# Rope, turns, values and the v0 bank in the attention loop of a hybrid decoder layer

## The chip, the cores and the metric

The kernel runs on one core of a Trainium2 chip. The core has five engines that work side by side and meet through semaphores: TensorE (PE in the profile, with its weight loads as PEld), VectorE (DVE), ScalarE (ACT), GpSimd (POOL) and SyncE (SP), whose queue issues the DMAs here. Matmuls and transposes write to PSUM, a memory of eight banks of 128 x 512 fp32; the other data lies in SBUF. The metric is the time of one execution on the device in microseconds (us).

## The reference

One layer of a hybrid decoder, all in fp32, for one sequence of 512 positions and a model width of 1024:

```python
h = rms_norm(x, norm_w)
u_s, z_s, q, k, v, z_a, r_s, r_a = split(h @ w_in)        # 1024 x 9216
y_s = s5_branch(u_s, ...)                                  # complex diagonal state space, GELU, GLU
y_s = (y_s * silu(z_s)) @ w_ssm_out
q = rope(rms_norm(q, q_norm_w)); k = rope(rms_norm(k, k_norm_w))   # 3 groups x 8 heads x 64
y_a = dilated_attention(q, k, v)       # windows 128, 512, 2048 at dilations 1, 4, 16
y_a = (y_a * silu(z_a)) @ w_attn_out
m = sigmoid(r_s) * y_s + sigmoid(r_a) * y_a
x = x + m @ w_o
```

The rope turns the first 16 of the 64 elements of each head of q and k: halves x1, x2 become x1 cos - x2 sin and x2 cos + x1 sin. The three groups' attention outputs are combined by their softmax denominators.

## The kernel before

**Matmuls.** fp32 accuracy comes from splitting both operands into a rounded part (`hi`) and a rest (`lo`) and making three matmuls, hi x hi, hi x lo and lo x hi (`mm3`, lines 62 to 65). Weights come from HBM by `load_w` (from line 183): SP's queue loads a piece, ACT rounds it to `w_hi` (line 108), DVE subtracts it to `w_lo` (line 110). There are two buffers of raw weights and three each of `w_hi` and `w_lo`; `get_w` hands out the next piece of a fixed list and starts the load of the piece two further on.

**Before the loop**, up to about 397 us: the norm of x, the state space branch, gates, and the projections by w_glu and w_ssm_out. Then the attention, by pairs of heads (`hp`, 0 to 3), each with its three groups.

**The loop** (from line 1094) does for each pair `hp`:

- `scores`: score matmuls in banks `sps`, softmax on DVE and ACT (lines 929 and 931), the merge of the groups' statistics, with small copies on POOL (lines 961 and 978), and the scaling of the probabilities `Pt` on DVE (line 985).
- `qk_first` for the next pair: a granule, that is `wide_granule` (line 817), q and k of groups 0 and 1 by 1024 rows of weights in four quarters. A quarter `kq` takes one piece of weights and runs four blocks, one for each 128 positions `r`, of six matmuls each into the four accumulators `pj`. The granule's result is copied to `raws` by ACT and goes through `qk_norm` (line 834): root mean square and scaling on DVE (line 846, 1024 elements a group), then the rope, four operations on POOL for each group (lines 852 to 857).
- `qk_second`: a second granule, q and k of group 2 and v of groups 1 and 2. Its callback `mid(kq)` runs in front of each quarter: in front of the second, `qk_turn` of group 0; in front of the third, `qk_turn` of group 1 (inside `queued()`); in front of the last, `values` of the present pair. The accumulators are emptied by ACT (lines 903, 905, squares at 879).
- `v0_unit`: v of group 0 for the next pair, 24 matmuls into an accumulator `pj`, then a copy `vt`; then `qk_turn` of group 2, and the transposes of `vt` (`finv`).

The last pair has no next one: it runs gate projections (`ra_unit`) and its `values`.

**A turn** (`qk_turn`, line 859) makes the transposed q (a = 0) and k (a = 1) of a group: for each of q and k four transposes of 128 x 128 into one bank `qtp`, which ACT copies to the rounded part (line 873) and DVE to the rest (line 874); the bank comes free behind both. For k of groups 1 and 2 the copies are made in two halves of 64 partitions.

**`values`** (line 988) takes the pair's probabilities in four steps: for each of the two heads, up to four transposes into a bank `ptp` and a copy of it to SBUF, `ptb`, by ACT for the first head (line 1027) and by DVE for the second (line 1029); then, one step behind, 16 matmuls of 128 columns into the bank `ot`. Together 30 transposes and 60 matmuls.

**PSUM** in this part (lines 1041 to 1043): four accumulators `pj` (pool `ps_p`), three banks for turns, scores, `ptp` and the transposes of v0 (pool `ps_g`, function `bank`), one for `ot`.

**Order.** A planner orders the instructions of each engine when the program is built, by the order in which the program names them and a model of their costs; an instruction that isn't ready by the model lets later ones pass. Each engine then runs its list in that fixed order. `queued()` (line 69) ties the instructions traced inside it, on PE, behind the PE instruction traced last.

Of the kernel before, what the change touches and what calls it, by code (L numbers as in the profile page):

```python
# [2 lines left out]

# [1 line left out]

# [6 lines left out]
F32 = mybir.dt.float32  # L12
# [3 lines left out]
ALU = mybir.AluOpType  # L16
# [17 lines left out]
NP = 4  # L34
# [18 lines left out]
def tile_hybrid_block(ctx: ExitStack, tc: tile.TileContext, x, positions, norm_w, w_in, lam_re, lam_im,  # L53
# [15 lines left out]
    def queued():  # L69

        return tc.issue_after(last[0].ins)
# [28 lines left out]
    def bank(name):  # L100
        return ps_g.tile([P, 512], F32, name=name, tag="g")
# [90 lines left out]
        split(hi, lo, raw, lo_eng=lo_w[0])  # L192
        return hi, lo

    def cm_unit(rh, rl, kts=KT):
        hi, lo = get_w()
        ps = ps_p.tile([P, 512], F32, name="pj", tag="pj")
        for k in range(kts):
            mm3(ps, hi[:, k], lo[:, k], rh[:, k], rl[:, k], k == 0, k == kts - 1)
        return ps  # L200
# [380 lines left out]
                            hi[:, k], lo[:, k], kh == 0 and k == 0 and rr == 0, kh == 1 and k == 3)  # L581
        return pss

    def v0_unit(hp, V):
        ps = cm_unit(hT_hi, hT_lo)
        vt = t2k("vt")
        act.copy(vt.rearrange("p (b r j) -> p r b j", r=4, b=4), ps.rearrange("p (r b j) -> p r b j", r=4, b=4))

        def finish():
            pt = bank("vtp")  # L590
            for b in range(NB):
                pe.transpose(pt[:, b * P:(b + 1) * P], vt[:, b * P:(b + 1) * P], ident)
            act.copy(V[:, 0].rearrange("p b c -> p (b c)"), pt)
        return finish
# [219 lines left out]
    if "gT" in dbg:  # L814
        sp.dma_start(dbg["gT"], gT_hi.bitcast(F32).rearrange("p k s -> p (k s)"))

    def wide_granule(th, tl, mid=None):

        pss = [ps_p.tile([P, 512], F32, name="pj", tag="pj") for _ in range(NB)]
        for kq in range(4):  # L820
            if mid:
                mid(kq)
            hi, lo = get_w()
            for r in range(NB):
                for k in range(2):
                    kk = 2 * kq + k
                    mm3(pss[r], th[:, kk, r * P:(r + 1) * P], tl[:, kk, r * P:(r + 1) * P], hi[:, k], lo[:, k],
                        kk == 0, kk == KT - 1)
        return pss

    def new_raw(i):
# [2 lines left out]
    def qk_norm(gs, raws, sq):  # L834

        n = 4 * len(gs)
        v = sml.tile([P, 32], F32, name="qv", bufs=1)[:, 0:NB * n]
        rstd = sml.tile([P, 32], F32, name="qrstd", bufs=1)[:, 0:NB * n]
        qa = sml.tile([P, 32], F32, name="qa", bufs=1)[:, 0:NB * n]
        qb = sml.tile([P, 32], F32, name="qb", bufs=1)[:, 0:NB * n]  # L840
        dve.tensor_scalar(v.rearrange("p (r h) -> p r h", r=NB), sq, 1.0 / HD, EPS, op0=ALU.mult, op1=ALU.add)
        rsqrt(rstd, v, [P, NB * n], qa, qb)
        rs = rstd.rearrange("p (r h) -> p r h", r=NB)
        for i, (g, raw) in enumerate(zip(gs, raws)):
            rv = raw.rearrange("p r (h d) -> p r h d", h=4)
            dve.tensor_tensor(rv, rv, rs[:, :, 4 * i:4 * i + 4].unsqueeze(3).broadcast_to([P, NB, 4, HD]), op=ALU.mult)  # L846
            t1 = sml.tile([P, NB * 2, 2, 16], F32, name="rt1", bufs=1)
            t2 = sml.tile([P, NB * 2, 2, 16], F32, name="rt2", bufs=1)
            rh = raw.rearrange("p r (a h d) -> p (r a) h d", a=2, h=2)
            cv = tC[:, g].rearrange("p r a d -> p (r a) d").unsqueeze(2)  # L850
            sv = tS[:, g].rearrange("p r a d -> p (r a) d").unsqueeze(2)
            pool.tensor_tensor(t1, rh[:, :, :, 0:16], cv.broadcast_to([P, NB * 2, 2, 16]), op=ALU.mult)  # L852
            pool.tensor_tensor(t2[:, :, :, 0:8], rh[:, :, :, 8:16],
                               sv[:, :, :, 0:8].broadcast_to([P, NB * 2, 2, 8]), op=ALU.mult)
            pool.tensor_tensor(t2[:, :, :, 8:16], rh[:, :, :, 0:8],
                               sv[:, :, :, 8:16].broadcast_to([P, NB * 2, 2, 8]), op=ALU.mult)
            pool.tensor_tensor(rh[:, :, :, 0:16], t1, t2, op=ALU.add)

    def qk_turn(g, raw, QT, KA, KB):
        for a in range(2):  # L860
            ps = bank("qtp")
            pn = ps.rearrange("p (b r j) -> p r b j", r=4, b=4)
            for r in range(NB):
                o = pn[:, r] if g == 0 else ps[:, r * P:(r + 1) * P]
                pe.transpose(o, raw[:, r, a * P:(a + 1) * P], ident)
            if a == 0 or g == 0:
                parts = [(slice(0, P), QT[0][:, g], QT[1][:, g]) if a == 0 else (slice(0, P), KA[0], KA[1])]
            else:
                parts = [(slice(64 * h, 64 * h + 64), KB[0][64 * h:64 * h + 64, g - 1, h],
                          KB[1][64 * h:64 * h + 64, g - 1, h]) for h in range(2)]  # L870
            for sl, hi, lo in parts:
                w = wcol[sl, g, a:a + 1]
                act.activation(hi, ps[sl], AF.Copy, scale=w)  # L873
                dve.scalar_tensor_tensor(lo, ps[sl], w, hi.bitcast(F32), op0=ALU.mult, op1=ALU.subtract)  # L874
# [18 lines left out]
        qk_norm((0, 1), raws, sq)  # L893
        return raws

    def qk_second(hp, mid=None):

        pss = wide_granule(hT_hi, hT_lo, mid)
        raw = new_raw(0)
        V = new_v()  # L900
        sq = sml.tile([P, NB, 8], F32, name="ssq")[:, :, 0:4]
        for r in range(NB):
            act.copy(raw[:, r], pss[r][:, 0:256])
            squares(sq[:, r], pss[r][:, 0:256])
            act.copy(V[:, 1:3, r], pss[r][:, 256:512].rearrange("p (g c) -> p g c", g=2))  # L905
        qk_norm((2,), [raw], sq)
        return raw, V
# [80 lines left out]
    def values(hp, Pt, V):  # L988
        ot = ps_o.tile([P, 512], F32, name="ot", tag="o")
        ov = ot.rearrange("d (r b j) -> d b r j", r=4, b=4)  # L990
        pend = []

        def pv(kind, bb, pts):
            for i in range(2):
                b = 2 * bb + i
                for k in range(2):
                    if kind == 0 and b == 0 and k == 0:
                        continue
                    for h in range(2):
                        po = slice(64 * h, 64 * h + 64)  # L1000
                        if kind == 0:
                            v = V[:, 0, b - 1 + k, po]
                            o = ov[po, b]
                        else:
                            v = V[:, 1 + k, b, po]
                            o = ot[po, b * P:(b + 1) * P]
                        first = kind == 0 and b == 0
                        pe.matmul(o, v, pts[h][:, (2 * i + k) * P:(2 * i + k + 1) * P], start=first,
                                  stop=kind == 1 and b == NB - 1 and k == 1, skip_group_check=True)

        n = 0
        for kind in range(2):
            for bb in range(2):
                pts = []
                k0 = 1 if kind == 0 and bb == 0 else 0
                for h in range(2):
                    ps = bank("ptp")
                    for i in range(2):
                        for k in range(2):
                            if 2 * i + k < k0:  # L1020
                                continue
                            pe.transpose(ps[:, (2 * i + k) * P:(2 * i + k + 1) * P],
                                         Pt[:, h, kind, 2 * bb + i, k * P:(k + 1) * P], ident)
                    pt = PT[n % 4]
                    n += 1
                    if h == 0:
                        act.copy(pt[:, k0 * P:], ps[:, k0 * P:])
                    else:
                        dve.tensor_copy(pt[:, k0 * P:], ps[:, k0 * P:])
                    pts.append(pt)  # L1030
                pend.append((kind, bb, pts))
                if len(pend) > 1:
                    pv(*pend.pop(0))
        pv(*pend.pop(0))
        at = t2k("at")
        dve.scalar_tensor_tensor(at, ot, 0.5, sza[:, hp], op0=ALU.mult, op1=ALU.mult)
        split(aT[:, 0, hp], aT[:, 1, hp], at, lo_eng=pool)
# [56 lines left out]
    for hp in range(NP):  # L1094
        Pt = scores(hp, *QK)
        if hp < NP - 1:
            raws = qk_first()

            def mid(kq):
                if kq == 1:  # L1100
                    qk_turn(0, raws[0], *QK)
                if kq == 2:
                    with queued():
                        qk_turn(1, raws[1], *QK)
                if kq == 3:
                    values(hp, Pt, V)

            raw, V_next = qk_second(hp + 1, mid)
            V = V_next
            finv = v0_unit(hp + 1, V)  # L1110
            qk_turn(2, raw, *QK)
            finv()
        else:
# [68 lines left out]
```

## Time and profile before

| what | value |
|---|---|
| median of 3 runs | 728.95 us (727.94 to 730.92) |
| profiled execution | 727.79 us |
| its span, first to last instruction | 726.0 us |
| mean granted TensorE clock | 0.991 |
| busy PE, DVE, ACT, POOL | 691.6, 455.4, 314.6, 190.9 us |
| HBM read and written | 68.46 and 10.49 MB |

A row of a timeline gives start, duration of the run of instructions, engine, line, operation, tile written and tiles read, shapes and count; in brackets the engine's idle time before it and who ended it. A row of a window gives its length and, for PE, PEld, DVE, ACT and POOL, busy us and (in brackets) instructions, then the granted PE clock, the DMA engines' busy share and GB/s. A row of groups gives count, busy us, mean ns of one, and the engine's idle time before them. A row of waits gives us in total, times, longest. Matmuls are pipelined, so their durations overlap: what one costs in a stream is the distance of starts.

### The profile page before, as it was taken

What the parts mean: (1) busy time and instruction counts of PE and PEld (TensorE: products, weight loads), DVE (VectorE), ACT (ScalarE), POOL (GpSimd) and SP (SyncE); (2) the same over time, 40 slices, a digit from 0 to 9 for tenths busy, and PEclk for the clock granted to TensorE, in tenths of its full rate; (3) what the DMA queues carried; (4) which work ended last, traced back from release to release, by engine and by line L of the source; (5) the groups of instructions that cost most, each with busy time, mean ns of one, the idle gap of its engine ahead of it and who ended that gap; (6) DMA issues with size and microseconds to landing.
All of it is one profiled execution on the core that took longest, in us unless ns stands there. A gap on an engine that the chain in (4) does not pass through costs nothing.

```text
span 726.0 us, 12680 instructions
## 1 busy us (share of the span) xinstructions
PE 691.6 (95%) x4821; PEld 574.3 (79%) x4821; DVE 455.4 (63%) x912; ACT 314.6 (43%) x631; POOL 190.9 (26%) x346
## 2 busy tenths in 40 slices
PE   2799799999999999999999999999989998999997
PEld 2787687788978887888889888788868877888886
DVE  6859663999956645764325659755764667464832
ACT  6433453332326465442144456537253725443320
POOL 3426540140205343450000326121601160230000
PEclk9999899999999999999999999999999999999999
DMA  8433652564546544455333432322312231327441
GB/s 206 106 99 93 169 135 79 142 159 132 122 131 147 127 105 138 129 166 185 95 102 94 131 88 63 84 59 59 115 32 60 62 112 30 116 74 249 130 145 58
DMA packets 137213, 82.14 MB, mean 113 GB/s; under 512 B 32696, under 2 KB 125632, under 8 KB 137024
## 3 DMA queue, kind: packets, MB, share of 16 engines
q1 hardware_dynamic: 135088, 78.96, 38.0%
q0 software_dynamic: 2048, 2.36, 2.6%
q8 instruction: 38, 0.62, 0.4%
q14 instruction: 23, 0.19, 0.1%
q10 hardware_dynamic: 16, 0.00, 0.0%
HBM read 68.46 MB, written 10.49 MB: 109 GB/s over the span
## 4 chain that ended last, share of the span: by engine, by line
PE 89%; DVE 3%; ACT 2%; SPq 2%; DMA 2%; issue 1%; ACTq 0%
PE pj L63 73%; PE sps L63 3%; PE yps L63 3%; PE ot L63 2%; PE ptp L67 2%; PE kps L63 2%; PE xps L63 1%; DMA Uj<-ud 1%; PE qtp L67 1%; SPq L443 1%; PE wps L67 1%; DVE w_lo L110 1%; DMA w_raw<-in_w_in_dram 1%; ACT qkp L873 1%; SPq L219 1%; ACT w_hi L108 1%
## 5 line engine op out<-in xcount | busy, mean ns | idle before, releaser
L108 ACT ACTIVATE w_hi<-w_raw 128x1024 fp32r<-128x1024 f32 x100 | 106.1, 1062 | 231.8 <-PE pj L63 197.4
L110 DVE TENSOR_TENSOR w_lo<-w_raw,w_hi 128x1024 fp32r<-128x1024 f32 x98 | 124.5, 1271 | 106.5 <-ACT w_hi L108 106.0
L63 PE MATMUL pj<-hT_lo,w_hi 128*128 128x512 f32 (+1 forms) x344 | 130.9, 381 | 3.6 <-DVE hT_lo L252 3.6
L63 PE MATMUL pj<-hT_hi,w_hi 128*128 128x512 f32 (+1 forms) x344 | 130.8, 383 | 2.0 <-ACT V L905 1.4
L63 PE MATMUL pj<-hT_hi,w_lo 128*128 128x512 f32 (+1 forms) x344 | 130.7, 381 | 1.6 <-DVE w_lo L110 1.6
L63 PE MATMUL pj<-w_hi,hT_hi 128*128 128x512 f32 (+1 forms) x288 | 105.6, 368 | 0.0
L63 PE MATMUL pj<-w_lo,hT_hi 128*128 128x512 f32 (+1 forms) x288 | 105.6, 367 | 0.0
L63 PE MATMUL pj<-w_hi,hT_lo 128*128 128x512 f32 (+1 forms) x288 | 105.2, 368 | 0.0
L63 PEld LDWEIGHTS pj<-hT_lo,w_hi 128*128 128x128 f32 x344 | 65.5, 190 | 15.6 <-DVE hT_lo L252 4.5
L63 PEld LDWEIGHTS pj<-hT_hi,w_lo 128*128 128x128 f32 x344 | 65.5, 190 | 14.4 <-DVE w_lo L110 2.6
L63 PEld LDWEIGHTS pj<-hT_hi,w_hi 128*128 128x128 f32 x344 | 65.1, 191 | 14.5 <-ACT V L905 2.1
L63 PEld LDWEIGHTS pj<-w_hi,hT_lo 128*128 128x128 f32 x288 | 54.3, 189 | 8.8
L63 PEld LDWEIGHTS pj<-w_hi,hT_hi 128*128 128x128 f32 x288 | 54.3, 189 | 8.8 <-issue 0.2
L63 PEld LDWEIGHTS pj<-w_lo,hT_hi 128*128 128x128 f32 x288 | 54.4, 189 | 8.6
L931 ACT ACTIVATE Pt<-Pt,st 128x256 f32<-128x256 f32 (+1 forms) x64 | 31.0, 492 | 18.4 <-DVE st L929 18.4
L852 POOL TENSOR_TENSOR rt<-qraw,tC 128x256 f32<-128x256 f32 x12 | 14.1, 1175 | 86.8 <-DVE qraw L846 86.5
L735 POOL TENSOR_TENSOR kt<-kt,dg 16x128 f32<-16x128 f32 x8 | 4.8, 597 | 120.7 <-ACT kt L734 116.2
L739 POOL DMA_DIRECT2D dd<-kt x64 | 33.7, 535 | 2.4 <-POOL kt L735 2.4
L874 DVE SCALAR_TENSOR_TENSOR qkp<-qtp,wcol,qkp 128x512 fp32r<-128x512 f32 (+1 forms) x32 | 23.0, 746 | 12.7 <-ACT qkp L873 12.7
L961 POOL COPY sw<-st 32x4 f32<-32x4 f32 x64 | 12.0, 187 | 71.4 <-ACT Pt L931 68.6
L873 ACT ACTIVATE qkp<-qtp,wcol 128x512 fp32r<-128x512 f32 (+1 forms) x32 | 20.8, 685 | 15.2 <-PE qtp L67 10.0
L278 POOL TENSOR_TENSOR ab<-dd,AT 128x512 f32<-128x512 f32 x16 | 22.0, 1385 | 14.1 <-DVE ab L279 14.1
(263 smaller groups left out, 1289.0 us busy)
## 6 DMA issues: line engine op xcount, KB each, us to landing
w_raw<-in_w_in_dram SPq DMA_DIRECT2D x40, 512.0 KB
w_raw<-in_w_in_dram SPq DMA_DIRECT2D x112, 128.0 KB
w_raw<-in_w_glu_dram SPq DMA_DIRECT2D x8, 512.0 KB
w_raw<-in_w_ssm_out_dram SPq DMA_DIRECT2D x8, 512.0 KB
w_raw<-in_w_o_dram SPq DMA_DIRECT2D x8, 512.0 KB
x_all<-in_x_dram SPq DMA_DIRECT2D x4, 512.0 KB
ud<-uT SPq DMA_DIRECT2D x8, 256.0 KB
Uj<-ud SPq DMA_DIRECT2D x8, 256.0 KB
```

Of the source, the lines that this page charges most:

```text
L63: last[0] = nc.tensor.matmul(*a, **k)
L67: last[0] = nc.tensor.transpose(*a, **k)
L108: act.activation(hi, src, AF.Copy, scale=scale)
L110: e.tensor_tensor(lo, src, hi.bitcast(F32), op=ALU.subtract)
L219: sp.dma_start(x_t[r], xv[r])
L278: eng.tensor_tensor(tv, a2.unsqueeze(2).broadcast_to(sh), ai, op=ALU.mult)
L739: pool.dma_start(M[Q * t:Q * t + Q, :, 0:P - Q * t], kt[:, :, t:].rearrange("q g k p -> q g (k p)"))
L852: pool.tensor_tensor(t1, rh[:, :, :, 0:16], cv.broadcast_to([P, NB * 2, 2, 16]), op=ALU.mult)
L873: act.activation(hi, ps[sl], AF.Copy, scale=w)
L874: dve.scalar_tensor_tensor(lo, ps[sl], w, hi.bitcast(F32), op0=ALU.mult, op1=ALU.subtract)
L931: act.activation(o, o, AF.Exp, bias=nm, scale=-1.0, accum_out=st[:, kind, 1, h, b:b + 1])
L961: pool.tensor_copy(sw[32 * r:32 * r + 32, :, :, b], st[32 * b:32 * b + 32, 1, :, :, r])
```

## The change

Five things change in the loop.

1. The four rope operations go from POOL to DVE, in all groups.
2. `wide_granule` calls `mid(kq, r)` in front of every block instead of every quarter, and a new callback `after(kq, r)` behind it. When `mid` says so, the block's matmuls are tied behind the PE instruction traced last.
3. The turns of groups 0 and 1 are each cut into their q and k: q of group 0 stands in front of the third quarter's last block, k of group 0, q of group 1 and k of group 1 in front of the last quarter's first, second and third block. Each is tied behind the PE instruction in front of it, and the block behind it is tied too.
4. `values` is traced behind the second quarter's last block instead of in front of the last quarter. For all pairs but the last, ACT makes both heads' copies to `ptb`.
5. `v0_unit` in the loop accumulates in a bank of the turns' pool instead of an accumulator `pj`.

```diff
-    def cm_unit(rh, rl, kts=KT):
+    def cm_unit(rh, rl, kts=KT, ps=None):
         hi, lo = get_w()
-        ps = ps_p.tile([P, 512], F32, name="pj", tag="pj")
+        if ps is None:
+            ps = ps_p.tile([P, 512], F32, name="pj", tag="pj")
...
-    def wide_granule(th, tl, mid=None):
+    def wide_granule(th, tl, mid=None, after=None):
...
         for kq in range(4):
-            if mid:
-                mid(kq)
             hi, lo = get_w()
             for r in range(NB):
-                for k in range(2):
-                    kk = 2 * kq + k
-                    mm3(pss[r], th[:, kk, r * P:(r + 1) * P], tl[:, kk, r * P:(r + 1) * P], hi[:, k], lo[:, k],
-                        kk == 0, kk == KT - 1)
+                tied = mid(kq, r) if mid else False
+                with queued() if tied else nullcontext():
+                    for k in range(2):
+                        kk = 2 * kq + k
+                        mm3(pss[r], th[:, kk, r * P:(r + 1) * P], tl[:, kk, r * P:(r + 1) * P], hi[:, k], lo[:, k],
+                            kk == 0, kk == KT - 1)
+                if after:
+                    after(kq, r)
...
-            pool.tensor_tensor(t1, rh[:, :, :, 0:16], cv.broadcast_to([P, NB * 2, 2, 16]), op=ALU.mult)
+            dve.tensor_tensor(t1, rh[:, :, :, 0:16], cv.broadcast_to([P, NB * 2, 2, 16]), op=ALU.mult)
...
-    def qk_turn(g, raw, QT, KA, KB):
-        for a in range(2):
+    def qk_turn(g, raw, QT, KA, KB, turned=(0, 1)):
+        for a in turned:
...
-                    if h == 0:
+                    if h == 0 or hp < NP - 1:
                         act.copy(pt[:, k0 * P:], ps[:, k0 * P:])
...
-            def mid(kq):
-                if kq == 1:
-                    qk_turn(0, raws[0], *QK)
-                if kq == 2:
-                    with queued():
-                        qk_turn(1, raws[1], *QK)
-                if kq == 3:
+            steps = {(2, 3): (0, 0), (3, 0): (0, 1), (3, 1): (1, 0), (3, 2): (1, 1)}
+
+            def mid(kq, r):
+                if (kq, r) not in steps:
+                    return False
+                g, a = steps[kq, r]
+                with queued():
+                    qk_turn(g, raws[g], *QK, turned=(a,))
+                return True
+
+            def after(kq, r):
+                if (kq, r) == (1, 3):
                     values(hp, Pt, V)
 
-            raw, V_next = qk_second(hp + 1, mid)
+            raw, V_next = qk_second(hp + 1, mid, after)
             V = V_next
-            finv = v0_unit(hp + 1, V)
+            finv = v0_unit(hp + 1, V, bank("v0p"))
```

More of the change, by code (lines that the diff above doesn't have):

```diff
@@ L1 @@
 import math
-from contextlib import ExitStack
+from contextlib import ExitStack, nullcontext
 import numpy as np
@@ L582, in tok_granule, with v0_unit @@
         return pss
-    def v0_unit(hp, V):
-        ps = cm_unit(hT_hi, hT_lo)
+    def v0_unit(hp, V, ps=None):
+        ps = cm_unit(hT_hi, hT_lo, ps=ps)
         vt = t2k("vt")
@@ L851, in qk_norm @@
             sv = tS[:, g].rearrange("p r a d -> p (r a) d").unsqueeze(2)
-            pool.tensor_tensor(t1, rh[:, :, :, 0:16], cv.broadcast_to([P, NB * 2, 2, 16]), op=ALU.mult)
-            pool.tensor_tensor(t2[:, :, :, 0:8], rh[:, :, :, 8:16],
+            dve.tensor_tensor(t1, rh[:, :, :, 0:16], cv.broadcast_to([P, NB * 2, 2, 16]), op=ALU.mult)
+            dve.tensor_tensor(t2[:, :, :, 0:8], rh[:, :, :, 8:16],
                                sv[:, :, :, 0:8].broadcast_to([P, NB * 2, 2, 8]), op=ALU.mult)
-            pool.tensor_tensor(t2[:, :, :, 8:16], rh[:, :, :, 0:8],
+            dve.tensor_tensor(t2[:, :, :, 8:16], rh[:, :, :, 0:8],
                                sv[:, :, :, 8:16].broadcast_to([P, NB * 2, 2, 8]), op=ALU.mult)
-            pool.tensor_tensor(rh[:, :, :, 0:16], t1, t2, op=ALU.add)
-    def qk_turn(g, raw, QT, KA, KB):
-        for a in range(2):
+            dve.tensor_tensor(rh[:, :, :, 0:16], t1, t2, op=ALU.add)
+    def qk_turn(g, raw, QT, KA, KB, turned=(0, 1)):
+        for a in turned:
             ps = bank("qtp")
@@ L894, in qk_first, with qk_second @@
         return raws
-    def qk_second(hp, mid=None):
-        pss = wide_granule(hT_hi, hT_lo, mid)
+    def qk_second(hp, mid, after):
+        pss = wide_granule(hT_hi, hT_lo, mid, after)
         raw = new_raw(0)
```

## The prediction

> **What bounds the kernel now.** I read the page's busy times and chain first, then what TensorE (PE) waited for in the stretch of the attention loop, 398 to 662 us from the span's start.
>
> ```profile
> span 726.0 us, 12680 instructions
> PE 89%; DVE 3%; ACT 2%; SPq 2%; DMA 2%; issue 1%; ACTq 0%
> PE qtp L67 <- DVE qkp L874: 3.5, 2, 1.8
> PE pj L63 <- ACT V L905: 1.4, 3, 0.5
> PE ptp L67 <- DVE qkp L874: 1.0, 2, 0.5
> 520.00:590.00 70.00, 67.28 (x380) 55.02 (x379) 41.73 (x113) 33.50 (x81) 18.02 (x45) 0.98 0.23 66
> ```
>
> PE makes 89% of the chain that ended last, so only what PE stops doing, or stops waiting for, shortens the kernel. The three rows of waits (us in total, times, longest) are all that PE waited for in the loop: 5.9 us. The last row is 70 us of the second head pair: PE busy 67.28, VectorE (DVE) 41.73, ScalarE (ACT) 33.50, GpSimd (POOL) 18.02. The change moves work between engines with room and moves PE's waits; it removes no matmul. Its worth must lie in those waits and in what they cause.
>
> Next, the timeline of PE in the loop's second and third head pairs, from the first turn transpose (`qtp`) to the first matmul of the granule's last quarter.
>
> ```profile
> 525.92 1.47 PE L67 MATMUL qtp<-ident,qraw 128*128 128x128 f32 x12
> ...
> 541.05 0.50 PE L63 MATMUL pj<-hT_hi,w_hi 128*128 128x512 f32 x1 [0.47 <-ACT V L905]
> 596.69 1.47 PE L67 MATMUL qtp<-ident,qraw 128*128 128x128 f32 x12
> 599.92 0.66 PE L67 MATMUL qtp<-ident,qraw 128*128 128x128 f32 x4 [1.76 <-DVE qkp L874]
> 600.58 0.55 PE L67 MATMUL ptp<-ident,Pt 128*128 128x128 f32 x3
> 601.61 0.98 PE L67 MATMUL ptp<-ident,Pt 128*128 128x128 f32 x7 [0.48 <-DVE qkp L874]
> ...
> 607.34 1.97 PE L63 MATMUL ot<-ptb,V 128*64 128x128 f32 x32
> 609.78 0.50 PE L63 MATMUL pj<-hT_hi,w_hi 128*128 128x512 f32 x1 [0.47 <-ACT V L905]
> ```
>
> Sixteen turn transposes and all of `values` stand in one heap. There are three banks: the turns fill them, the fourth turn waits 1.76 us for a bank, `values` waits 0.48 us for the next, and the last quarter 0.47 us for its accumulators. The bank is late because of what stood in front on ACT and DVE:
>
> ```profile
> 596.88 1.06 ACT L108 ACTIVATE w_hi<-w_raw 128x1024 fp32r<-128x1024 f32 x1 [4.33 <-PE pj L63]
> 597.98 1.23 DVE L110 TENSOR_TENSOR w_lo<-w_raw,w_hi 128x1024 fp32r<-128x1024 f32 x1 [4.15 <-ACT w_hi L108]
> 599.12 1.40 DVE L874 SCALAR_TENSOR_TENSOR qkp<-qtp,wcol,qkp 128x512 fp32r<-128x512 f32 x2
> ```
>
> A weight split took ACT 1.06 us and DVE 1.23 us just when the turn's copies were due. The first head pair doesn't show the heap: there matmuls of the granule lie between turns and `values`, and only the 0.5 us for V remains.
>
> **What the heap costs.** From the chain in order of time:
>
> ```profile
> 451.01 0.87 PE qtp L67 x8
> 505.18 20.91 PE pj L63 x91
> ```
>
> A turn transpose costs 0.87/8 = 0.109 us, a projection matmul 20.91/91 = 0.23. Third pair: 609.78 - 596.69 = 13.09 us from first turn to next matmul. Its work is 16 x 0.109 = 1.74, plus `values`: three transposes (0.33) and 601.61 to 609.31 (7.70), 8.03. Left: 13.09 - 1.74 - 8.03 = **3.3 us**, slightly more than the waits' 2.7, as the pipe refills after each. The second pair takes 541.05 - 525.92 = 15.13, **2.0 us** more with the same waits. Windows of 1 us show why (the column with 0.50, 0.59 and 1.00 is PE's granted clock):
>
> ```profile
> 532.00:533.00 1.00, 1.00 (x5) 0.64 (x5) 0.76 (x1) 0.74 (x2) 0.00 (x0) 0.50 0.00 0
> 534.00:535.00 1.00, 1.00 (x10) 0.83 (x6) 0.50 (x1) 0.00 (x0) 0.00 (x0) 0.59 0.03 8
> 602.00:603.00 1.00, 1.00 (x9) 0.66 (x8) 0.80 (x3) 0.74 (x2) 0.00 (x0) 1.00 0.08 23
> ```
>
> After the waits the clock fell to half for a few us; after the same waits in the third pair it didn't. The heaps together lose 3.3 + 3.3 + 2.0, and 0.5 in the first pair: 9.1 us.
>
> **The change, part by part.** *Turns between blocks.* A block of a quarter is six matmuls, 6 x 0.23 = 1.4 us; with a turn's four transposes (0.44) a new bank is asked for every 1.8 us, and the same bank after three turns, 5.4 us. A turn's copies:
>
> ```profile
> L873 ACT ACTIVATE qkp<-qtp,wcol 128x512 fp32r<-128x512 f32 x16 | 10.6, 690 | 8.5 <-PE qtp L67 8.5
> L874 DVE SCALAR_TENSOR_TENSOR qkp<-qtp,wcol,qkp 128x512 fp32r<-128x512 f32 x16 | 11.6, 745 | 6.3 <-ACT qkp L873 6.3
> L403 DVE TENSOR_TENSOR pw<-pw 64x256 f32<-64x256 f32 x1 | 0.4, 410 | 0.0
> L535 DVE TENSOR_TENSOR maskB<-maskB 128x128 f32<-128x128 f32 x1 | 0.3, 293 | 0.0
> L846 DVE TENSOR_TENSOR qraw<-qraw,qrstd 128x1024 f32<-128x1024 f32 x12 | 14.3, 1223 | 0.7 <-DVE qrstd L120 0.2
> L852 POOL TENSOR_TENSOR rt<-qraw,tC 128x256 f32<-128x256 f32 x12 | 14.1, 1175 | 86.8 <-DVE qraw L846 86.5
> L1027 ACT COPY ptb<-ptp 128x512 f32<-128x512 f32 x12 | 7.0, 586 | 13.3 <-PE ptp L67 13.2
> L1029 DVE COPY ptb<-ptp 128x512 f32<-128x512 f32 x12 | 8.3, 691 | 10.9 <-PE ptp L67 10.9
> L1029 DVE COPY ptb<-ptp 128x384 f32<-128x384 f32 x4 | 2.2, 552 | 0.4 <-PE ptp L67 0.4
> ```
>
> 0.69 + 0.75 = 1.4 us (twice that for the halved last one), and a weight split in front adds 2.3: 3.7 against 5.4. The bank waits of second and third pair go. The tie holds the matmuls behind each turn, so a turn whose input is late now stops PE; that is weighed below.
>
> *Rope on VectorE.* Per group two operations of 256 and two of 128 elements. DVE's nearest rows, 64x256 at 410 and 128x128 at 293 ns, give 2 x 0.41 + 2 x 0.29 = 1.4 us; bounds 1.2 (four of the short row) and 4.9 (four of L846's 1223 ns). POOL needs 1175 ns for its first alone. So two groups take 2.8 us on DVE. It queues in front of weight splits, softmax and the row statistics there. PE uses a split two quarters later, 24 x 0.23 = 5.5 us each, and SP's next weight load, which waits for that `w_lo`, has the same cover. Cost: none. POOL loses the rope and its copies of softmax statistics are no longer behind it; SP's queue gets and loses nothing.
>
> *Copies by ScalarE.* Per pair DVE gives up 0.55 + 3 x 0.69 = 2.6 us and takes 3 x 1.4 = 4.2 of rope: +1.6 on 41.7 in 70. ACT takes four more copies, some 0.59 us each. The two copies of a step now come one after the other, behind them the next weight split. PE's work per step (7.7/4 = 1.9 us) exceeds two copies (1.2), so only the first step shows: between nothing (granule matmuls fill it) and split plus copy, 1.06 + 0.59 = 1.65 us. The row nearest, the first pair, has such fill and shows no idle PE, the other pairs none either with both engines copying; I take the middle, **0.8 us** a pair, 2.4 in all; bounds 0 to 5.
>
> *`values` a quarter earlier.* It needs the scaled probabilities:
>
> ```profile
> 515.34 0.62 DVE L985 TENSOR_SCALAR Pt<-Pt,sfb 128x256 f32<-128x256 f32 x2
> 456.46 0.60 DVE L985 TENSOR_SCALAR Pt<-Pt,sfb 128x256 f32<-128x256 f32 x2
> 453.01 7.31 PE pj L63 x32
> ```
>
> The third quarter of the second pair ended at 526.1 (505.18 + 20.91) and so began at 520.6: 4.6 us after the last scaling. In the first pair scaling ends at 457.1. There the third quarter's 24 matmuls are the last 20 of the 32 up to 460.3 and four singles behind: it began at 460.3 - 20 x 0.23 = 455.7, and without the twelve turn transposes ahead of it (1.3 us) begins near 454.4, before the scaling's end. But `values` starts with the part scaled first, and the blocks in front of the first turn aren't tied and can fill 18 x 0.23 = 4.1 us. Cost zero, at worst 3 us once.
>
> *v0 in a turn's bank.* The wait on V (0.47 three times, in the 9.1) goes.
>
> ```profile
> 476.81 0.57 ACT L587 COPY vt<-pj 128x512 f32<-128x512 f32 x1
> 483.52 0.87 PE qtp L67 x8
> 518.19 2.36 DVE L846 TENSOR_TENSOR qraw<-qraw,qrstd 128x1024 f32<-128x1024 f32 x2
> ```
>
> The bank is held 24 x 0.23 + 0.57 = 6 us; the next to ask for banks is the third group's turn, 483.5 in the first pair, when the copy of v0 had ended at 477.4. Cost nothing; if that cover went, the turn would wait for the 0.57 us copy.
>
> [...]
>
> **Sum.** 9.1 regained - 2.4 of new waits = 6.7. Span 726.0 - 6.7 = 719.3; the profiled execution took 727.8, 1.8 more than its span, so 721.1. It lay 1.2 below the median of the runs shown; I leave that in the range. Forecast **721**, with 716.5 to 725 its own range: with no new wait 718.7, with another 2 us of pipe refills inside `values` 716.7.
>
> **Rivals.** *ScalarE becomes late.* The upper bound holds: 5 us of new waits, and the first pair's 3: 726.0 - 9.1 + 8 + 1.8 = **726.7**. For it: ACT runs in order and a split was in its way twice already. Against: it is busy under half of 70 us. Chance 0.12.
>
> [...] Chance 0.06.
>
> *`values` stays behind.* It isn't tied; the planner may issue it where it stood. The turns are still spread; the 0.48 us and its refill (0.3) in front of `values` stay in two pairs, so 7.5 of the 9.1 return: 726.0 - 7.5 + 2.4 + 1.8 = **723**. Chance 0.12.
>
> *The rope is late for the tied turns: slower.* The first turn stands in front of the third quarter's last block. If `values` isn't in front, PE is there at 520.6 + 4.1 = 524.7. DVE's normalisation began at 518.19 (the row above) and rope would end at 518.2 + 2.4 + 2.8 = 523.4. The margin is 1.3 us, 9 with `values` in front. If DVE's queue puts splits and copies between, PE stops at a tied turn. From 1.3 + 3 us late in each pair it eats the gain; with 7 us, 5.7 past the margin, the sum is 726.0 - 9.1 + 3 x 5.7 + 1.8 = **736**. DVE's share (42 of 70) speaks against it. Chance 0.10.
>
> **Chances.** Forecast 0.60. What this kernel's measurement can tell from no change is about 0.5%, 3.6 us: below 725.3 is faster. Forecast and `values` behind: 0.72 faster. The two cases near 727: 0.18 same. Slower 0.10. The range takes in the forecast's own, the cases at 723, 726.7 and 727.1, and the median's 1.2 above the profiled run in part: 716.5 to 728.
>
> **What would show it.** Right: PE waits for L874 and L905 gone in the loop, turns in fours between six matmuls, granted clock 1.00 throughout, rope near 1.4 us a group on DVE. Wrong: new PE waits on `ptb` (copies late), on `qraw` (rope late), on `Pt` (scaling late), or idle PE beyond 3 us in the loop.

## The result, and the profile after

| kernel | median | executions | ratio to before, 95% interval |
|---|---|---|---|
| before | 729.08 us (727.1 to 731.48) | 8 | 1 |
| changed | 724.49 us (721.61 to 726.27) | 8 | 0.9934 [0.9911, 0.9957] |

The change gains 4.6 us, 0.7%. Forecast was 721, a gain of 8. The profiled execution of the changed kernel took 726.27 us, the longest of the eight; its span is 724.5, only 1.5 less than before's. Part of that is lost ahead of the attention, where PE's last wait, for a copy of ACT, ends 1.7 us later than before. From the timelines of before and of the changed kernel, in that order:

```profile
281.96 0.50 PE L63 MATMUL pj<-gT_hi,w_hi 128*128 128x512 f32 x1 [0.99 <-ACT gs L776]
```

```profile
283.69 0.50 PE L63 MATMUL pj<-gT_hi,w_hi 128*128 128x512 f32 x1 [0.99 <-ACT gs L777]
```

In a second profile of the changed kernel (the last experiment) it ends at 282.02, so this differs between executions. It makes a common zero for comparing profiles: from there to the end it is 444.0 us before and 440.8 in both profiles of the changed kernel, 3.2 us less. The medians' 4.6 is more; the three fastest executions, 721.6 to 722.2 us, were not profiled.

Now PE's waits in the attention loop, 398 to 662 us (us in total, times, longest): the three rows of before are gone, and there is one new row, the only one.

```profile
PE ptp L67 <- DVE Pt L988: 1.9, 2, 1.6
```

Then the chain in order of time, around the third head pair of the changed kernel (start, us, what):

```profile
592.35 0.44 PE ptp L67 x4
592.78 0.81 PE ot L63 x12
593.59 1.02 PE ptp L67 x8
594.61 1.02 PE ot L63 x16
595.64 1.02 PE ptp L67 x8
596.66 1.03 PE ot L63 x16
597.69 0.58 PE qtp L67 x4
598.27 1.39 PE pj L63 x6
599.67 0.36 PE ot L63 x2
600.03 0.58 PE qtp L67 x4
600.62 1.02 PE ot L63 x14
601.63 1.59 PE pj L63 x6
603.22 0.44 PE qtp L67 x4
603.66 1.38 PE pj L63 x6
605.04 0.44 PE qtp L67 x4
605.48 2.74 PE pj L63 x12
```

That is the order the change asks for: `values`, then turns in fours with blocks of six between them (the last 16 matmuls of `values` fall in among the first two turns), each piece starting where the last ends. PE waits for no bank here.

How long does a pair take? The turn of group 2 (`qtp` x8) comes once per pair, so the distance from one to the next is the length of a pair. From the chains of before and of the changed kernel, in that order:

```profile
424.66 0.87 PE qtp L67 x8
483.52 0.87 PE qtp L67 x8
554.29 0.87 PE qtp L67 x8
623.02 0.87 PE qtp L67 x8
```

```profile
427.94 0.87 PE qtp L67 x8
490.57 0.87 PE qtp L67 x8
556.31 0.87 PE qtp L67 x8
622.05 0.87 PE qtp L67 x8
```

Second pair 70.77 to 65.74 us, third 68.73 to 65.74: **5.0 and 3.0 us gained**. First pair 58.86 to 62.63, and that with fewer matmuls in it, as windows of the projection matmuls alone show (the number behind x; 24 of v0 come on top in the changed kernel):

```profile
424.60:483.45 58.85, 44.43 (x185) 33.81 (x184) 0.00 (x0) 9.09 (x25) 1.00 0.26 72
```

```profile
427.90:490.50 62.60, 38.16 (x158) 28.76 (x157) 0.00 (x0) 8.15 (x24) 0.97 0.21 62
```

185 before, 158 + 24 = 182 after: three matmuls (0.7 us) fewer, so the first pair **loses 3.8 + 0.7 = 4.5 us**. What it loses them on, in the timeline of PE and DVE of the changed kernel:

```profile
451.36 1.32 PE L63 MATMUL sps<-qkp 64*128 64x256 f32 x12
456.32 0.70 PE L67 MATMUL ptp<-ident,Pt 128*128 128x128 f32 x3 [1.60 <-DVE Pt L988]
457.31 1.01 PE L67 MATMUL ptp<-ident,Pt 128*128 128x128 f32 x5 [0.28 <-DVE Pt L988]
```

```profile
455.98 2.06 DVE L988 TENSOR_SCALAR Pt<-Pt,sd 128x128 f32<-128x128 f32 x8
457.96 1.13 DVE L988 TENSOR_SCALAR Pt<-Pt,sfb 128x256 f32<-128x256 f32 x4
```

The pair's last score matmuls start at 451.36 (before: 443.86, chain row "443.86 1.25 PE sps L63 x12"), the scaling of their probabilities at 455.98, and `values` stands in PE's list behind the scores with only eight granule matmuls between them. PE waits 1.9 us, and after that its clock falls:

```profile
457.00:458.00 1.00, 0.72 (x6) 0.61 (x5) 1.00 (x6) 0.48 (x1) 0.86 (x4) 0.84 0.00 0
458.00:459.00 1.00, 1.00 (x5) 0.42 (x4) 1.00 (x5) 0.59 (x1) 0.82 (x5) 0.50 0.00 0
460.00:461.00 1.00, 1.00 (x6) 0.86 (x5) 0.62 (x3) 0.63 (x2) 0.24 (x2) 0.50 0.00 0
461.00:462.00 1.00, 1.00 (x13) 0.66 (x11) 0.00 (x0) 0.10 (x2) 0.00 (x0) 0.95 0.00 0
```

The shares of 0.84 and 0.95 put the half clock from 457.7 to 461.1, 3.4 us. Half of it, 1.7 us, is the estimate of what that costs: a transpose took 0.23 us from 458.87 on, at clock 0.50, against 0.13 from 464.09 on, at 1.00. Waits and clock make 3.6 of the 4.5; no row shows the rest by itself. That a wait costs more than its idle time, as the prediction has it, stays an estimate from its 3.3 against 2.7 us.

### The profile page after: what moved, and what is told of

It is laid out like the page before. It is cut to its first block, busy times and chain, and to the rows that moved or that the text cites. A ratio compares the mean times of both kernels' runs of the same rounds, so it can differ in the third digit from the quotient of the medians.

```text
span 724.5 us, 12667 instructions
## 1 busy us (share of the span) xinstructions
PE 694.0 (96%) x4821; PEld 575.5 (79%) x4821; DVE 457.2 (63%) x948; ACT 320.3 (44%) x643; POOL 151.4 (21%) x298
## 4 chain that ended last, share of the span: by engine, by line
PE 88%; DVE 4%; DMA 3%; SPq 2%; ACT 2%; issue 1%; ACTq 0%
PE pj L63 69%; PE sps L63 3%; PE yps L63 3%; PE ot L63 2%; PE v0p L63 2%; PE ptp L67 2%; DMA w_raw<-in_w_in_dram 2%; PE kps L63 2%; PE qtp L67 2%; PE xps L63 1%; DMA Uj<-ud 1%; SPq L444 1%; PE wps L67 1%; DVE w_lo L110 1%; SPq L220 1%
## 5 line engine op out<-in xcount | busy, mean ns | idle before, releaser
L110 DVE TENSOR_TENSOR w_lo<-w_raw,w_hi 128x1024 fp32r<-128x1024 f32 x98 | 122.1, 1245 | 92.3 <-ACT w_hi L108 92.2
L63 PE MATMUL pj<-hT_lo,w_hi 128*128 128x512 f32 (+1 forms) x320 | 122.4, 383 | 3.7 <-DVE hT_lo L253 3.7
L63 PE MATMUL pj<-hT_hi,w_lo 128*128 128x512 f32 (+1 forms) x320 | 121.6, 381 | 1.7 <-DVE w_lo L110 1.7
L63 PE MATMUL pj<-hT_hi,w_hi 128*128 128x512 f32 (+1 forms) x320 | 122.1, 385 | 0.7 <-ACT w_hi L108 0.7
L63 PE MATMUL pj<-w_hi,hT_hi 128*128 128x512 f32 (+1 forms) x288 | 107.1, 373 | 0.0
L63 PE MATMUL pj<-w_lo,hT_hi 128*128 128x512 f32 (+1 forms) x288 | 106.0, 368 | 0.0
L63 PE MATMUL pj<-w_hi,hT_lo 128*128 128x512 f32 (+1 forms) x288 | 105.1, 368 | 0.0
L63 PEld LDWEIGHTS pj<-hT_lo,w_hi 128*128 128x128 f32 x320 | 61.9, 193 | 14.9 <-DVE hT_lo L253 4.6
L63 PEld LDWEIGHTS pj<-hT_hi,w_lo 128*128 128x128 f32 x320 | 61.7, 193 | 13.3 <-DVE w_lo L110 2.7
L63 PEld LDWEIGHTS pj<-hT_hi,w_hi 128*128 128x128 f32 x320 | 61.3, 193 | 12.0 <-ACT w_hi L108 0.9
L63 PEld LDWEIGHTS pj<-w_hi,hT_hi 128*128 128x128 f32 x288 | 54.4, 189 | 9.1 <-issue 0.7
L63 PEld LDWEIGHTS pj<-w_hi,hT_lo 128*128 128x128 f32 x288 | 54.4, 189 | 8.8
L63 PEld LDWEIGHTS pj<-w_lo,hT_hi 128*128 128x128 f32 x288 | 54.4, 189 | 8.2
L63 PE MATMUL pj<-gT_hi,w_hi 128*128 128x512 f32 x64 | 24.7, 391 | 1.0 <-ACT gs L777 1.0
```

What stands on the lines that cost most here:

```text
L63: last[0] = nc.tensor.matmul(*a, **k)
L110: e.tensor_tensor(lo, src, hi.bitcast(F32), op=ALU.subtract)
```

## The experiments

Theory A: the missing gain went into the first pair, where `values` meets probabilities that aren't scaled yet. Rivals: ScalarE's copies one after the other, or the rope on VectorE, in every pair. Ratios are to the kernel before on the same chip. PE's order, where it is named below, is that of the traces. Lengths from the common zero are from the end of PE's last wait ahead of the attention, as above.

**The first pair's `values` a quarter later.**

```diff
-                if (kq, r) == (1, 3):
+                if (kq, r) == ((2, 3) if hp == 0 else (1, 3)):
                     values(hp, Pt, V)
```

> The changed kernel, but in the first head pair `values` is traced behind the third quarter instead of the second. Theory A (the first pair pays: `values` stands in PE's list before its probabilities are scaled; PE idle 1.9 us, then half clock for 3.4 us, some 4 us in all): the waits of `ptp` on `Pt` go, pairs two and three stay as they are, 720.5 us, ratio to the kernel before 0.988. Rival B (the missing gain lies in ScalarE's copies or in rope on VectorE, in every pair): no change, 724.5, ratio 0.993.

719.72 us, ratio 0.988 [0.9859, 0.99]. PE's waits in the loop are gone altogether; the stretch that held them reads (PE busy 18.93 of 19.00, clock 1.00):

```profile
451.00:470.00 19.00, 18.93 (x146) 15.39 (x145) 11.71 (x36) 12.44 (x32) 6.04 (x17) 1.00 0.19 54
```

Theory A stands: moving one call in one pair brings back some 4 us by the ratios (0.9934 to 0.988) and 4.8 us from the common zero (440.8 to 436.1). The kernel is better than both given ones.

**Rope back on POOL.**

```diff
-            dve.tensor_tensor(t1, rh[:, :, :, 0:16], ...)
+            pool.tensor_tensor(t1, rh[:, :, :, 0:16], ...)
```

(all four operations)

> The changed kernel with the four rope operations back on POOL. Theory A in a stricter form (rope in VectorE's queue is what brought the first pair's last scores behind 27 instead of 16 granule matmuls, and so the scaling behind `values`): the scores stand earlier, first pair's waits go or shrink below 0.5 us, 720 to 721, ratio 0.988. Rival B: rope on VectorE is needed for the tied turns; with POOL's 4 to 6 us for two groups PE waits on `qraw` in front of the third quarter's last block, 726 or more.

720.88 us, 0.9891 [0.9867, 0.9915]; no PE wait in the loop. In its list the first pair's last scores stand behind 16 granule matmuls, as before, and not behind 27 as in the changed kernel, and 34 matmuls, not 8, lie between them and `values`. From the common zero, PE is ready for `values` at the same time in both kernels (170.9 us here, 171.0 in the changed one), but the last scores start at 161.8 against 167.7 and the scaling at 169.7 against 172.3. So the rope's move to VectorE is what brought the scores 5.9 us and the scaling 2.6 us later, and `values` met it. How much of the 2.6 is the planner's order and how much the rope's own time in VectorE's queue isn't parted. POOL's rope isn't late for the tied turns.

**Copies on both engines again; v0 in an accumulator again.** Two runs, each the changed kernel with one line undone:

```diff
-                    if h == 0 or hp < NP - 1:
+                    if h == 0:
```

```diff
-            finv = v0_unit(hp + 1, V, bank("v0p"))
+            finv = v0_unit(hp + 1, V)
```

> The changed kernel with the second head's `ptb` copies back on VectorE. Theory A: pairs two and three show no PE wait with ScalarE alone, so nothing moves: 724.5, ratio 0.993 to 0.994. Rival (the prediction's term of 0.8 us a pair for copies one after the other): 2.4 us faster, 722, ratio 0.990.

> The changed kernel with v0 again in one of the four accumulators. If the bank is what removed the wait of 0.47 us on the copy of V: it returns three times, 726, ratio 0.995. If the earlier `values` removed it (ScalarE's copies of V no longer stand behind `ptb` copies): nothing moves, 724.5.

Copies: 725.74, 0.9963 [0.9945, 0.998], no gain, rather a loss that its interval doesn't part from the changed kernel's; a wait of `ot` on VectorE's copy, 0.7 us, is new in the first pair, and the half clock there lasts from 458.3 to 465.1, twice as long as in the changed kernel (mean granted clock from 451 to 520 us 0.95, against 0.98). v0: 724.78, 0.9942 [0.9917, 0.9966], as the changed kernel; PE waits for no copy of V. The bank is worth nothing. Why the wait went is in ACT's waits of before, in the loop (us in total, times, longest):

```profile
ACT V L905 <- PE ot L63: 4.3, 3, 1.4
```

The copy of the new V overwrites the V that `values` reads, so it waits for the last `ot` matmuls; it wasn't ScalarE's own copies for `values` that held it, as the expectation has it. Before, the whole granule had run ahead of `values`, and v0, next on PE, then waited 0.47 us for that copy to empty its accumulator. Now tied blocks of the granule stand behind `values`: in this run's third pair the first copy of V ends at 602.6, and v0 starts at 606.5. The earlier place of `values` isn't needed for that: the run with spread turns alone, below, has v0 in an accumulator too and no such wait.

**Which part dissolves the heap?** Theory C: spreading the turns carries the whole gain. Four runs: whole turns in their old places with the rest changed; `values` behind the third quarter in all pairs; the kernel before with spread turns (and `values` behind the third quarter); the kernel before with the rope on VectorE.

```diff
-            steps = {(2, 3): (0, 0), (3, 0): (0, 1), (3, 1): (1, 0), (3, 2): (1, 1)}
-
             def mid(kq, r):
-                if (kq, r) not in steps:
-                    return False
-                g, a = steps[kq, r]
-                with queued():
-                    qk_turn(g, raws[g], *QK, turned=(a,))
-                return True
+                if (kq, r) == (1, 0):
+                    qk_turn(0, raws[0], *QK)
+                if (kq, r) == (2, 0):
+                    with queued():
+                        qk_turn(1, raws[1], *QK)
+                return False
```

> The changed kernel with the turns of groups 0 and 1 whole again and not spread: group 0 in front of the second quarter, untied, group 1 in front of the third, tied; `values`, rope, copies and v0's bank stay changed. Theory C (spreading the turns is what removes the waits for banks in pairs two and three): eight turn transposes stand in front of `values` again, PE waits for banks some 1 to 2.2 us in each of these pairs, and the first pair's loss stays or moves: 726 us, ratio 0.997. Rival D (moving `values` away from the turns is enough): no bank waits in pairs two and three, 724.5 or less, ratio 0.993.

```diff
-                if (kq, r) == (1, 3):
+                if (kq, r) == (2, 3):
```

> The changed kernel with `values` traced behind the third quarter in all pairs. Theory A: as the run that did this for the first pair alone, 719.7 us, ratio 0.988, since the spread turns keep the banks free wherever `values` stands. Rival (the earlier `values` is needed in pairs two and three): bank waits or half clock come back there, 2 to 5 us more, 722 to 725.

```diff
+            steps = {(2, 3): (0, 0), (3, 0): (0, 1), (3, 1): (1, 0), (3, 2): (1, 1)}
...
+                if (kq, r) == (2, 3):
+                    values(hp, Pt, V)
```

> The kernel before with the split and tied turns of the change, and `values` traced one block behind the third quarter; rope on POOL, copies on both engines, v0 in an accumulator, all as before. Theory C: the turns carry the whole gain, 720 us, ratio 0.989. Rival: rope on POOL is late for the tied turns or the accumulator's wait (0.47 us a pair) stays, 722 to 727.

```diff
-            pool.tensor_tensor(t1, rh[:, :, :, 0:16], ...)
+            dve.tensor_tensor(t1, rh[:, :, :, 0:16], ...)
```

> The kernel before with only the rope on VectorE. Theory C: heaps of turns and `values` and their bank waits of 2.2 us stay in pairs two and three, with half clock in some executions, and the first pair has enough granule matmuls in front of `values` to hide later scores: 727 to 728, ratio 0.998 to 1.0. Rival (rope's delay on POOL made the turns late and so the heap): the heap dissolves, 722 to 724.

| run | median | ratio | PE's largest wait in the loop |
|---|---|---|---|
| turns whole | 724.72 | 0.9951 [0.9931, 0.9971] | `ptp` on a turn's bank, 3.7 us in two waits |
| `values` later everywhere | 725.47 | 0.9955 [0.9937, 0.9973] | `qtp` on rope (DVE), 4.8 us in two waits |
| spread turns alone | 728.58 | 0.9983 [0.9961, 1.0004] | `qtp` on rope (POOL), 5.1 us in two waits |
| rope alone | 731.07 | 1.0028 [1.0006, 1.005] | `qtp` on a turn's bank, 3.5 us in two waits |

Theory C fell. Spread turns alone do free the banks (0.2 us of bank waits are left in the loop, of 4.5 before), but they gain nothing that is clear of noise, since they then wait for the rope. In the run with `values` later everywhere, second pair:

```profile
519.74 0.42 DVE L855 TENSOR_TENSOR rt<-qraw,tC 128x256 f32<-128x256 f32 x1
520.60 0.42 DVE L860 TENSOR_TENSOR qraw<-rt,rt 128x256 f32<-128x256 f32 x1
521.08 0.66 PE L67 MATMUL qtp<-ident,qraw 128*128 128x128 f32 x4 [2.42 <-DVE qraw L860]
```

The tied turn starts 0.06 us after the rope's last addition and has waited 2.42 us for it; everything behind it on PE waits too. In the run with whole turns the waits for banks are back, 1.87 us in the second pair:

```profile
526.08 1.03 PE L67 MATMUL qtp<-ident,qraw 128*128 128x128 f32 x8
526.96 0.49 PE L67 MATMUL ptp<-ident,Pt 128*128 128x128 f32 x3
529.32 1.35 PE L67 MATMUL ptp<-ident,Pt 128*128 128x128 f32 x7 [1.87 <-DVE qkp L877]
```

Behind this heap come eight more `qtp` and then v0: with no blocks tied, the planner again let the whole granule pass, and the earlier place of `values` in the source isn't an earlier place on PE. So spread turns free the banks, and `values` in front of them gives the rope the time that the tie takes away. Spreading alone gains nothing, and the earlier trace of `values` with whole turns (and the other three parts) somewhat under half. No run has the earlier `values` by itself. The rope's move by itself gains nothing either and rather costs 0.3%, since the heap stays.

**What is needed.** Theory E: these two, with the first pair's scaling in time; copies and v0's bank nothing. The first run undoes copies and v0 in the kernel with the first pair's `values` later, the second in the kernel with rope on POOL, and the third is the changed kernel again on the same chip.

```diff
-                    if h == 0 or hp < NP - 1:
+                    if h == 0:
...
-            finv = v0_unit(hp + 1, V, bank("v0p"))
+            finv = v0_unit(hp + 1, V)
```

> The first experiment's kernel (first pair's `values` a quarter later) with two parts of the change undone: the second head's `ptb` copies on VectorE and v0 in an accumulator, as before. Theory E (what counts is turns between blocks with `values` in front of them, and in the first pair scaling done in time; copies and v0's bank are worth nothing): 720 us, ratio 0.988 to 0.990. Rival (the two undone parts hide waits that show once the first pair no longer waits, 0.5 us a pair each): 722 to 723.

> As the run with rope on POOL, and copies and v0 undone too: of the change only the spread turns and the earlier `values` are left. Theory E: 720.5 us, ratio 0.989. Rival (rope on VectorE, copies or v0's bank carry a part): 723 or more, with PE waits on `qraw`, `ptb` or the copy of V.

> The changed kernel once more, on the chip of these runs. Theory A and E: 724.5 us, ratio 0.993 to 0.994, so 4 us above both others; single executions without half clock in the first pair 2 us lower than those with it. Rival: no difference from the other two.

723.95 (0.9934 [0.9915, 0.9953]), **720.05 (0.9883 [0.9864, 0.9902])** and 723.96 (0.9943 [0.9923, 0.9963]). The second holds for Theory E; the first breaks its half about the copies: 4 us above the kernel whose copies ScalarE made. DVE and PE there, in the first pair:

```profile
459.57 0.60 DVE L988 TENSOR_SCALAR Pt<-Pt,sfb 128x256 f32<-128x256 f32 x2
460.48 0.62 DVE L988 TENSOR_SCALAR Pt<-Pt,sfb 128x256 f32<-128x256 f32 x2 [0.30 <-POOL sfb L981]
461.40 0.61 DVE L988 TENSOR_SCALAR Pt<-Pt,sfb 128x256 f32<-128x256 f32 x2 [0.31 <-POOL sfb L981]
461.93 1.15 DVE L1032 COPY ptb<-ptp 128x384 f32<-128x384 f32 x2
```

```profile
462.54 0.87 PE L63 MATMUL ot<-ptb,V 128*64 128x128 f32 x10 [2.13 <-DVE ptb L1032]
```

VectorE's copy for the first step of `values` stands in its queue behind the scaling for the last steps, which waits for POOL; PE waits 2.13 us, and half clock follows from 464.2 to 467.6 (granted clock 0.61 in the window from 464 us, 0.50 in the next). ScalarE's copies are worth something exactly where `values` runs while VectorE still scales, that is where the rope made the scaling late. With the rope on POOL a smaller wait of that kind is left (1.4 us, with no half clock behind it: 1.00 from 420 to 500 us), and the time is the best kernels' within the noise; from the common zero it is 437.9 us, against 436.1 for the first experiment's kernel. The third run's expectation for single executions stays open: its six lie from 721.84 to 726.01 us, and only one was profiled, which has the same waits and the same half clock as the changed kernel's first profile.

## Why the prediction was right in sign and too high in size

- *The time.* The median of 724.49 lies in the prediction's own range of 716.5 to 725, and that is partly luck. A term put at nothing cost 4.5 us, and the 2.4 us put down for ScalarE's copies, which never came, made up for half of it. Of the signs named beforehand, the waits on L874 and L905 went and turns stand in fours between blocks; but a PE wait on `Pt`, a sign of being wrong, came, and the clock was not 1.00 throughout (0.50 from 458 to 461 us).
- *PE's waits are the worth of it*: right. The three rows are gone, and second and third pairs gained 5.0 and 3.0 us; the sum had 5.3 (3.3 and the clock's 2.0) and 3.3 there, of which 0.8 each was to be given back.
- *Turns between blocks*: the bank waits went by the spreading, as worked out; but the spreading alone doesn't bring the gain (ratio 0.9983), since the rope is then late. The sum took the margin for the rope from `values` in front, and rightly.
- *Rope on VectorE, 1.4 us a group*: right in size, four operations of the changed kernel make 0.42 + 0.29 + 0.29 + 0.42 = 1.42:

```profile
L855 DVE TENSOR_TENSOR rt<-qraw,tC 128x256 f32<-128x256 f32 x12 | 5.1, 422 | 0.2
L856 DVE TENSOR_TENSOR rt<-qraw,tS 128x128 f32<-128x128 f32 x12 | 3.4, 285 | 0.0
```

  "Cost: none" was wrong: weight splits had cover, but the first pair's last scores and their scaling came later by it.
- *Copies by ScalarE, 0.8 us a pair*: no such wait showed in any pair. They cost nothing and hold back a wait of 2.1 us in one place. ScalarE didn't become late.
- *v0 in a turn's bank*: its cost is nothing, as said; but the 0.47 us that I gave to it go without it too, since tied blocks now stand between `values` and v0.
- *`values` a quarter earlier, "Cost zero, at worst 3 us once"*: **this step failed**. It cost 4.5 us once, more than its worst case, in waits of 1.9 us for the scaling and half clock behind them. Two readings led there. First, the matmuls behind the heap at 541.05 and 609.78 read `pj<-hT_hi,w_hi`; in the granule the operands stand the other way round (`w_hi,hT_hi`), so these are v0's, not the last quarter's: the planner had let the whole granule pass ahead of turns and `values`. The count says the same: with the 33 run just ahead of 483.52, PE ran 33 + 25 + 2 + 2 + 19 + 20 + 91 = 192 projection matmuls up to 526.1, two whole granules. So the third quarter of the second pair began near 526.1 - 48 x 0.23 = 515.1, not 520.6, and the scaling ended 0.9 us after it, not 4.6 us before. In the first pair the gap was not 3 but some 8 us (third quarter near 449, scaling's end 457.1). Second, the 18 untied matmuls that were to fill it were already spent: behind the first `ptp` of that pair only 30 are left, 24 of them tied (the last block isn't).
- *Rivals.* The slower one, rope late for tied turns with `values` not in front, didn't come in the changed kernel but is just what the runs with `values` later and spread turns alone showed, 2.4 to 2.5 us in each of the second and third pairs. `values` didn't stay behind: it runs where the change traces it.
- *The clock and the refills.* The 9.1 us counts the second pair's 2.0 us of half clock as regained with the waits; that it goes with them was my estimate. For that pair it held: in the changed kernel PE doesn't wait there, the granted clock is 1.00 (490.5 to 556.2 us), and it gained 2.0 us more than the third. No run shows what the case at 727.1 us, chance 0.06, adds up, 2.0 us of half clock in each of the three pairs: in the changed kernel it came in the first alone, behind waits of 1.6 and 0.28 us, and in the run with the first pair's `values` later, a heap of 30 transposes, at most 12 in a row, and 60 narrow matmuls ran from 455.6 to 463.9 without a wait at clock 1.00. No profile here shows a fall of the clock in the loop without a wait in front of it. Nor does a run show the 2 us of refills inside `values` that the range takes in: that heap, without a wait, took 8.3 us, against the 8.03 that the prediction found for `values` in the third pair without its waits.

## What to carry to other kernels

Before costing a moved step, find out from the operands and the count of instructions where the planner really ran the work around it; the order in the source isn't the order on the engine. A tie is a promise that its input is ready: look for what gives the input its time (here `values`) and try the parts of a change in pairs as well as singly, since spread turns and the earlier `values` were worth 8 us together, spread turns alone nothing clear of noise, and the earlier `values` with whole turns, which the planner ran late again, somewhat under half. Moving work to an engine with room can still cost where it changes what that engine, or the planner's picture of it, finishes last: here the rope's move brought the first pair's scaling 2.6 us later.

## What the hardware showed that was not expected

Behind two waits of 1.6 and 0.28 us PE's clock fell to half for 3.4 us, where the prediction had 1.00 throughout. It doesn't happen each time: none followed the 1.76 and 0.48 us in before's third pair (clock 1.00 from 590 to 660 us), nor either wait of 1.9 us in the run with whole turns (1.00 from 500 to 640), and with only the second of the two waits of 2.4 us, `values` later everywhere, did the clock fall (1.00 from 500 to 570, 0.98 from 570 to 640). In the run with the rope alone, which keeps both heaps, the twelve executions lie in two groups: six from 727.0 to 730.2 us at mean granted clocks of 0.992 to 0.995, six from 731.9 to 733.4 at 0.983 to 0.986. In the run with v0 in an accumulator the two fastest executions, 718.11 and 719.85 us, are those with a mean clock of 0.998; the other eight, 723.77 to 726.09, have 0.988 to 0.995. That is more than the 1.7 us estimated for one fall. Falls outside the loop differ too: before's profile has half clock from 33.1 to 36.5 and from 80.9 to 87.7 us, the changed kernel's from 34.4 to 41.3 and from 85.6 to 89.0, and the first experiment's profile has 1.00 from 398 to 655 us and still a mean clock of 0.995. The two were not profiled, so where the rest lies stays open.
